# Moving every second low-part subtraction of the first block's weights from VectorE to GpSimd, in a two-block transformer kernel

## The chip, the cores and the metric

The kernel runs on one core of one Trainium2 chip. The metric is the device time of one execution in microseconds (us). Times below are the median of three runs; the profile is of one more execution.

## The reference, cut to what matters

Two transformer blocks are applied to 256 tokens of width 2048, everything in float32. The first block has adaptive scale and shift vectors, a projection `w_in` into attention and a recurrent mixer, two mixer projections that are gated and merged, the output projection `w_out`, and a gated feed-forward part. The second block prepends 16 tokens and has an attention layer and a gated linear attention layer.

```python
mod = (c @ w_ada[l] + b_ada[l])[:, None, :]
shift1, scale1, gate1, shift2, scale2, gate2 = jnp.split(mod, N_MOD, axis=-1)
h = rmsnorm(x, g_pre_mix[l]) * (1.0 + scale1) + shift1
proj = h @ w_in[l]
...
y_a = sliding_window_attention(qa, ka, va, attn_sinks[l]) @ w_attn_proj[l]
o_h = hgrn2_recurrence(q_h, f_h, i_h, lb_table[l])
...
merged = jax.nn.sigmoid(gate_a) * y_a + jax.nn.sigmoid(gate_h) * y_h
y = merged @ w_out[l]
x = x + gate1 * rmsnorm(y, g_post_mix[l])
...
y = (jax.nn.silu(g_ffn) * u_ffn) @ w_ffn_out[l]
x = x + gate2 * rmsnorm(y, g_post_ffn[l])
```

Every `@` with a large weight is the part that the change touches; the second block's weights are handled in the same way but are not touched.

## The kernel before, in words

**Weights as two parts.** TensorE multiplies in the reduced format fp32r, so each product is made of three: weight high part times activation high part, high times low, low times high (`mm3`, line 390). The weights come as a list of chunks, mostly 128 x 1024 float32 (512 KB), in the order of use (`_plan`, line 116): 56 chunks `w_first` and 92 chunks `w_in` (together the input projection), 32 `w_proj` (both mixer projections), 32 `w_out`, then the feed-forward part and the second block. So there are 212 chunks up to the end of the first block's output projection. Each chunk goes through three steps:

- `dma_chunks` (line 347): a DMA on SP's queue into one of five `raw` buffers (`NRAW`, line 53).
- `split_hi` (line 355): ScalarE rounds the chunk into one of three `wh` buffers (`NSPLIT`, line 62).
- `split_lo` (line 365): VectorE subtracts `wh` from `raw` and writes the low part into one of three `wl` buffers (lines 371 and 372). This is the last reader of the `raw` buffer, which then is free for another DMA.

**How far ahead.** A chunk of eight 128-deep tiles is 24 matmuls on TensorE. After the matmuls of a chunk are written down, `later_chunks` (line 384) writes down the low part of the chunk two further on, the high part of the chunk three further on, and the load of the one after that. A `wh` or `wl` buffer is free when TensorE has done with the chunk three before. The `raw` buffers are shared: the pieces of `w_adat` (128 of 512 KB, the adaptive vectors that are not needed at once) are loaded into the same five buffers (`later_load`, line 756), and VectorE reduces each with one multiply with accumulation against a broadcast copy of `c` (`later_piece`, line 767), then a few operations of one column.

**The order of the work.** Every engine executes its instructions in the order in which they are written down. The program writes them down with the help of a small model of the engines (`Clock`, line 144; `Timed`, line 191): matmuls of the main products first, and after each chunk `bg_step` (line 421) adds steps of the background work (the recurrence, the attention, gates, normalisations) as long as the model's VectorE is less than 4 us and its ScalarE less than 3 us ahead of its TensorE. A piece of `w_adat` is taken at a fixed rate for each chunk: 0.7 in the rest of `w_in`, 0.55 in `w_proj`, 0.85 in `w_out` (`RATES`, line 72), until there are none left. In the model a subtraction of 1024 elements on VectorE counts 1.14 us.

**Stages in the trace.** About 12 to 212 us: `w_first` with the first adaptive vectors; to 545 us the rest of `w_in` with recurrence and attention beside it; 545 to 637 us `w_proj` (`proj`, line 1343: two chunks for each of 16 outputs, two gated products read from PSUM, an addition and a split into high and low part on VectorE); 637 to 732 us `w_out`; then the feed-forward part begins with the first call of `next_layer` (line 1413).

**GpSimd before.** It does a few memsets and casts in the first block (lines 651, 691, 886, 955), small DMAs of the attention in the second block, and three additions at the end: the last loop (lines 2183 to 2197) makes eight tiles of the output, 128 x 512 each; tiles at k = 0, 4, 8 and 12 are summed by TensorE and copied by ScalarE, tiles at k = 2, 6 and 10 are added by GpSimd (line 2194), the tile at k = 14 by VectorE (line 2196).

Of the kernel before, what the change touches and what calls it, by code (L numbers as in the profile page):

```python
# [7 lines left out]
F32 = mybir.dt.float32  # L8
# [4 lines left out]
ALU = mybir.AluOpType  # L13
# [7 lines left out]
KT = D // 128  # L21
# [94 lines left out]
def _plan(a):  # L116

    plan = [a["w_first"][i] for i in range(a["w_first"].shape[0])]
    for i in range(74 - G1):
        plan += _tile_chunks(a["w_in"][i], KT)  # L120
    for n in range(KT):
        plan += _tile_chunks(a["w_proj"][n], KT)
    for n in range(KT):
        plan += _tile_chunks(a["w_out"][n], KT)
    plan += [a["w_fwave"][k] for k in range(KT)]
    i = 0
    for gi, gn in enumerate(FGROUPS):
        for j in range(2 * gn - (GF if gi == 0 else 0)):
            plan += _tile_chunks(a["w_ffn_in"][i], KT)
            i += 1  # L130
        for n in range(KT):
            plan += _tile_chunks(a[f"w_ffn_out{gi}"][n], gn)
    for w, wout in (("attn", "attn"), ("gla", "gla")):
        plan += [a[f"{w}_wave"][k] for k in range(KT)]
        for i in range(a[f"{w}_w_in"].shape[0]):
            plan += _tile_chunks(a[f"{w}_w_in"][i], KT)
        outs = [_tile_chunks(a[f"{w}_w_out"][n], KT) for n in range(KT)]
        if w == "attn":
            outs[:3] = [list(t) for t in zip(*outs[:3])]
        plan += sum(outs, [])  # L140
    return plan


class Clock:


    def __init__(self):
        self.t = dict(pe=0.0, dve=0.0, act=0.0, dma=0.0, dmaq=0.0)
        self.uses = {}
        self.end = 0.0  # L150
        self.table = None
# [70 lines left out]
def body(ctx, tc, a, out, dbg=None):  # L222
    nc = tc.nc
# [14 lines left out]
    def taken(pool, n, tile):  # L238

        r = rings.setdefault(pool, [])  # L240
        r.append(tile.tensor.name)
        if len(r) > n:
            clock.follow(r[-1], r[-1 - n])
        return tile

    def bank(name):
        return ps.tile([128, 512], F32, tag="b", name=name)
# [34 lines left out]
    clock = Clock()  # L282
    TE = Timed(nc.tensor, clock, "pe", lambda n, kw: n / 2400.0 * (
        4.0 if "lhsT" in kw and kw["lhsT"].dtype == F32 else 1.0) + 0.0025 if n > 16 else 0.11)
    VE = Timed(nc.vector, clock, "dve", lambda n, kw: max(0.07 + n / 960.0, 0.13))
    SE = Timed(nc.scalar, clock, "act", lambda n, kw: 0.1 + n / 1200.0)
    SY = Timed(nc.sync, clock, "dma", lambda n, kw: n * 512 / 390e3)
    GQ = Timed(nc.gpsimd, clock, "dmaq", lambda n, kw: DMAQ)
    tt = VE.tensor_tensor
    stt = VE.scalar_tensor_tensor  # L290
    ts = VE.tensor_scalar
    act = SE.activation
# [46 lines left out]

    plan = _plan(a)  # L340
    raws, splits = {}, {}
    ptr = dict(dma=0, hi=0, lo=0, use=0, mod=0)

    def raw_tile(name):
# [10 lines left out]
    def split_hi(upto):  # L355
        while ptr["hi"] < min(upto, len(plan)):
            i = ptr["hi"]
            n = plan[i].shape[1]
            dma_chunks(i + 1)
            wh = taken("wh", NSPLIT, whp.tile([128, CW], F32R, tag="wh", name="wh"))  # L360
            SE.copy(wh[:, :n], raws[i][:, :n])
            splits[i] = [wh, None]
            ptr["hi"] += 1

    def split_lo(upto):
        while ptr["lo"] < min(upto, len(plan)):
            i = ptr["lo"]
            n = plan[i].shape[1]
            split_hi(i + 1)
            wl = taken("wl", NSPLIT, wlp.tile([128, CW], F32R, tag="wl", name="wl"))  # L370
            tt(out=wl[:, :n], in0=raws.pop(i)[:, :n], in1=splits[i][0][:, :n].bitcast(F32),
               op=ALU.subtract)
            splits[i][1] = wl
            ptr["lo"] += 1

    def next_chunk():

        i = ptr["use"]
        ptr["use"] += 1
        split_lo(i + 1)  # L380
        split_hi(i + NSPLIT)
        return splits.pop(i)
# [13 lines left out]


    bg = []
    st_ = dict(quota=0.0, rate=0.0)

    limits = {}

# [37 lines left out]
    def mark(key):  # L440
        done[key] = clock.end
# [138 lines left out]
    def row_sums(st, sq, T, first, last):  # L580

        for i, o in enumerate(blocks(T)):
            TE.matmul(st[:, i:i + 1], lhsT=sq[:, o:o + 128], rhs=ones[:, 0:1],
                             start=(first and i == 0), stop=last, skip_group_check=True)
# [34 lines left out]
    def rstd_sums(accs, T, width, root=True, warm=0):  # L619
        st = bank("st")  # L620
        for i, acc in enumerate(accs):
            row_sums(st, acc, T, i == 0, i == len(accs) - 1)
        return rstd_rows(st, T, width, root, warm)

    def now(gen):

        while True:
            try:
                next(gen)
            except StopIteration as e:  # L630
                return e.value
# [596 lines left out]
    for i in range(n0):  # L1228
        u = ada_use()
# [20 lines left out]
    for gi, g in enumerate(KG):  # L1250
# [3 lines left out]
        for c in range(nch):  # L1254
            wh, wl = next_chunk()
# [42 lines left out]
            while used < int(want + 1e-6):  # L1298
# [8 lines left out]
                for _ in range(burst):  # L1307
                    u = ada_use()
# [104 lines left out]
    def next_layer(y, yacc, Ty, ycol, Tx, xcol, G, T, evac):  # L1413


        rb = now(rstd_sums(yacc, Ty, D, warm=WARM[0]))
        keep_warm(WARM[1])
        later_chunks()
        st = bank("xst")
        accs = [bank("wave") for _ in range(G)]  # L1420
        t0 = T2 - Tx

        def begin(k):
            if k >= KT:
                return
            residual(rb, y, Ty, ycol, k)
            if k:
                SE.mul(hh[k][:, :Tx], x[k][:, t0:], xcol(k))
            else:
                ts(out=hh[k][:, :Tx], in0=x[k][:, t0:], scalar1=xcol(k), scalar2=None,  # L1430
                   op0=ALU.mult)
                begin_lo(k)
            sqs[k] = t1("sq", Tx)
            act(out=sqs[k], in_=x[k][:, t0:], func=AF.Square)

        def begin_lo(k):
            if k < KT:
                pair_lo(hh[k][:, :Tx], hl[k][:, :Tx], x[k][:, t0:], xcol(k))

        def norm():  # L1440
            c = t1("sq", Tx)
            SE.copy(c, st[:, :Tx])
            yield 0.0
            rx = yield from rstd_sums([c], Tx, 32 * D)
            SE.copy(r2[:, :Tx], rx[:, :Tx])
            mark("r2")
            yield 0.0
            for g in range(G):
                while not room(evac, g):
                    yield 0.0  # L1450
                evac(g, accs[g][:, :T])
                wave["left"] -= 1
                yield 0.0

        del done["r2"]
        wave.update(left=G, most=G + 1)
        sqs = {}
        begin(0)
        begin(1)
        for k in range(KT):  # L1460
            wh, wl = next_chunk()
            tiles_ = [(accs[g][:, :T], slice(g * 128, (g + 1) * 128)) for g in range(G)]
            h, l = hh[k][:, :T], hl[k][:, :T]
            if k == 0:
                for w, v in ((wh, h), (wl, h), (wh, l)):
                    for o, ks in tiles_:
                        TE.matmul(o, lhsT=w[:, ks], rhs=v, start=w is wh and v is h, stop=False)
            else:
                for o, ks in tiles_:
                    mm3(o, wh[:, ks], wl[:, ks], h, l, False, k == KT - 1)  # L1470

            for j in range(k - 3, k + 1) if k % 4 == 3 else ():
                q = slice(32 * (j % 4), 32 * (j % 4) + 32)
                TE.matmul(st[q, :Tx], lhsT=ones[:, 0:32], rhs=sqs.pop(j), start=(k == 3),
                          stop=(k == KT - 1), skip_group_check=True)
            if k == KT - 1:
                urgent.append(norm())
                next(urgent[0])
            later_chunks()
            begin_lo(k + 1)  # L1480
            begin(k + 2)
# [180 lines left out]
    def turned(t, u):  # L1662

        for i in range(4):
            o, s = 32 * i, 32 * (i ^ 1)
            GQ.dma_start(out=u[o:o + 32], in_=t[s:s + 32])

# [488 lines left out]
    for i in range(G2, len(seq3)):  # L2156
        f, n, real = seq3[i]
# [8 lines left out]
    def x_pair(k):  # L2166
        return xs[k // 4][:, k % 4 * T2:(k % 4 + 2) * T2].rearrange(
            "p (a t) -> p a t", a=2)[:, :, R]
# [14 lines left out]
    for k in range(0, KT, 2):  # L2183
        if k == 4:
            sum_x(12)
        u = fin[k // 4][:, k % 4 * S:(k % 4 + 2) * S].rearrange("p (a t) -> p a t", a=2)
        tt(out=u, in0=rb, in1=y.two(k), op=ALU.mult)
        put = SY
        if k in sums:
            TE.matmul(sums[k], lhsT=ident, rhs=u, start=False, stop=True)  # L2190
            SE.copy(u, sums[k])
            put = nc.scalar
        elif k < KT - 2:
            nc.gpsimd.tensor_tensor(out=u, in0=u, in1=x_pair(k), op=ALU.add)
        else:
            tt(out=u, in0=u, in1=x_pair(k), op=ALU.add)
        put.dma_start(out=out[k // 2], in_=u)
# [160 lines left out]
```

## Time and profile before

| | |
|---|---|
| three runs, median (lowest to highest) | 2410.94 us (2409.06 to 2410.99) |
| the profiled execution, its own time | 2412.66 us |
| its span, first to last instruction | 2410.9 us |
| mean granted TensorE clock, share of full | 0.997 |
| TensorE, VectorE, ScalarE, GpSimd busy, share of the span | 99%, 70%, 50%, 3% |

PE is TensorE's matmuls, PEld its weight loads, DVE is VectorE, ACT is ScalarE, POOL is GpSimd and SP the engine whose queue issues the loads. In every view a time is in us from the start of the span, unless it is marked ns. A duration includes the tail of an instruction, so neighbours on one engine overlap a little in the records. A wait is given to whoever came last.

### The profile page before, as it was taken

Reading aid. Unit: us, or ns where it says so; the run is one execution under the profiler, and the core shown is the slowest. Engines: PE = TensorE matmul, PEld = TensorE weight load, DVE = VectorE, ACT = ScalarE, POOL = GpSimd, SP = SyncE. Lnnn points to the kernel's source line nnn. Section 1 sums busy time; section 2 is a strip of 40 time slices with the busy share of each in tenths; the row PEclk is TensorE's granted clock in tenths of the full one; section 3 lists DMA queues with packets and bytes.
Section 4 is the critical chain, followed back from the end, with each engine's and each line's share of the span. In section 5 each row is a group of like instructions: output and inputs, shape, how many; then the busy total and the mean of one; then the engine's idle time right before and its main releaser. Section 6 shows DMA issues by size and latency. Waiting matters only on the chain.

```text
span 2410.9 us, 49102 instructions
## 1 busy us (share of the span) xinstructions
PE 2380.5 (99%) x20217; PEld 2340.4 (97%) x20217; DVE 1691.1 (70%) x2865; ACT 1196.4 (50%) x1939; POOL 66.5 (3%) x131
## 2 busy tenths in 40 slices
PE   8999999999999999999999999999999999999998
PEld 7999999999999999999999999999999999999997
DVE  4897978888867965566655556777777566788664
ACT  4345565444445544444433444545555456855443
POOL 0000000000000000000000000121110000000000
PEclk9999999999999999999999999999999999999999
DMA  9975668798884666666665555554444445544453
GB/s 400 373 291 172 232 202 267 244 315 288 302 297 156 212 225 228 219 219 224 229 211 185 186 173 168 174 166 140 146 143 154 158 148 174 160 138 143 159 183 114
DMA packets 143249, 501.33 MB, mean 208 GB/s; under 512 B 17088, under 2 KB 17856, under 8 KB 143024
## 3 DMA queue, kind: packets, MB, share of 16 engines
q1 hardware_dynamic: 138240, 492.11, 60.7%
q0 software_dynamic: 3072, 3.35, 0.4%
q8 instruction: 158, 2.59, 0.4%
q10 hardware_dynamic: 1712, 2.73, 0.3%
q14 instruction: 67, 0.55, 0.1%
HBM read 492.68 MB, written 2.10 MB: 205 GB/s over the span
## 4 chain that ended last, share of the span: by engine, by line
PE 94%; DVE 2%; DMA 2%; ACT 1%; issue 0%; ACTq 0%; SPq 0%; DVEq 0%
PE acc L216 77%; PE wave L216 5%; PE yp L216 4%; DMA araw<-in_w_adat 1%; PE hgs L216 1%; PE sc L216 1%; PE go L216 1%; DVE wl L216 1%; PE ada L216 1%; PE st L216 1%; PE o L216 1%; DVE araw L216 1%; PE tp L216 0%; PE asc L216 0%; PE gm L216 0%
## 5 line engine op out<-in xcount | busy, mean ns | idle before, releaser
L216 ACT CAST wh<-raw 128x1024 fp32r<-128x1024 f32 (+1 forms) x754 | 774.0, 1027 | 1084.7 <-PE acc L216 732.1
L216 DVE TENSOR_TENSOR wl<-raw,wh 128x1024 fp32r<-128x1024 f32 (+1 forms) x754 | 899.7, 1194 | 432.9 <-ACT wh L216 429.3
L216 PE MATMUL acc<-hh,wh 128*128 128x256 f32 (+2 forms) x3488 | 1003.7, 288 | 2.5 <-ACT hh L216 2.5
L216 PE MATMUL acc<-hh,wl 128*128 128x256 f32 (+2 forms) x3488 | 988.5, 284 | 3.3 <-DVE wl L216 3.3
L216 PE MATMUL acc<-hl,wh 128*128 128x256 f32 (+2 forms) x3488 | 988.0, 284 | 2.9 <-DVE hl L216 2.9
L216 PEld LDWEIGHTS acc<-hh,wh 128*128 128x128 f32 x3488 | 658.8, 189 | 11.0 <-issue 5.0
L216 PEld LDWEIGHTS acc<-hl,wh 128*128 128x128 f32 x3488 | 658.3, 189 | 4.5 <-DVE hl L216 3.5
L216 PEld LDWEIGHTS acc<-hh,wl 128*128 128x128 f32 x3488 | 658.6, 189 | 4.1 <-DVE wl L216 4.1
L216 PE MATMUL acc<-h2l,wh 128*128 128x256 f32 x1200 | 337.9, 282 | 0.0
L216 PE MATMUL acc<-h2h,wl 128*128 128x256 f32 x1200 | 337.6, 281 | 0.0
L216 PE MATMUL acc<-h2h,wh 128*128 128x256 f32 x1200 | 335.8, 280 | 0.0
L216 PEld LDWEIGHTS acc<-h2h,wl 128*128 128x128 f32 x1200 | 227.3, 189 | 0.0
L216 PEld LDWEIGHTS acc<-h2h,wh 128*128 128x128 f32 x1200 | 226.9, 189 | 0.0
L216 PEld LDWEIGHTS acc<-h2l,wh 128*128 128x128 f32 x1200 | 225.2, 188 | 0.0
L216 DVE SCALAR_TENSOR_TENSOR araw<-araw,cb 128x1024 f32<-128x1024 f32 x144 | 175.5, 1219 | 12.9 <-DMA araw<-in_w_adat 12.7
L216 PE MATMUL wave<-hl,wh 128*128 128x272 f32 (+1 forms) x288 | 82.1, 293 | 0.8 <-DVE hl L216 0.8
L216 PE MATMUL wave<-hh,wh 128*128 128x272 f32 (+1 forms) x288 | 81.3, 291 | 0.1
L216 PE MATMUL wave<-hh,wl 128*128 128x272 f32 (+1 forms) x288 | 80.1, 287 | 0.0
L216 PE MATMUL acc<-oph,wh 128*128 128x272 f32 x256 | 74.3, 290 | 0.0
L216 PE MATMUL acc<-oph,wl 128*128 128x272 f32 x256 | 74.1, 289 | 0.0
L216 PE MATMUL acc<-opl,wh 128*128 128x272 f32 x256 | 73.7, 288 | 0.0
L216 PE MATMUL acc<-gpl,wh 128*128 128x256 f32 x256 | 72.1, 282 | 0.0
(390 smaller groups left out, 2987.5 us busy)
## 6 DMA issues: line engine op xcount, KB each, us to landing
raw<-in_w_ffn_in SPq DMA_DIRECT2D x164, 512.0 KB, 4.3
araw<-in_w_adat SPq DMA_DIRECT2D x128, 512.0 KB, 4.8
raw<-in_w_in SPq DMA_DIRECT2D x92, 512.0 KB, 4.8
raw<-in_gla_w_in SPq DMA_DIRECT2D x86, 512.0 KB, 3.6
raw<-in_attn_w_in SPq DMA_DIRECT2D x84, 512.0 KB, 3.5
araw<-in_w_mod SPq DMA_DIRECT2D x64, 512.0 KB, 9.2
raw<-in_w_ffn_out SPq DMA_DIRECT2D x64, 512.0 KB, 4.3
raw<-in_w_first SPq DMA_DIRECT2D x56, 512.0 KB, 6.8
```

The source lines that it names most:

```text
L216: return f(*args, **kw)
```

## The change

The subtraction of `split_lo` goes to GpSimd for chunks with an odd number, as long as a flag is set; the flag is cleared at the head of `next_layer`, whose first call comes after `w_out`. The program's model gets a sixth clock, for GpSimd, with 0.1 us + n/420 (2.54 us for 1024 elements). In the last loop the three additions of GpSimd go to VectorE.

```diff
     def __init__(self):
-        self.t = dict(pe=0.0, dve=0.0, act=0.0, dma=0.0, dmaq=0.0)
+        self.t = dict(pe=0.0, dve=0.0, act=0.0, dma=0.0, dmaq=0.0, pool=0.0)
...
     GQ = Timed(nc.gpsimd, clock, "dmaq", lambda n, kw: DMAQ)
+    GP = Timed(nc.gpsimd, clock, "pool", lambda n, kw: 0.1 + n / 420.0)
...
     raws, splits = {}, {}
+    st_ = dict(quota=0.0, rate=0.0, share=True)
     ptr = dict(dma=0, hi=0, lo=0, use=0, mod=0)
...
             wl = taken("wl", NSPLIT, wlp.tile([128, CW], F32R, tag="wl", name="wl"))
-            tt(out=wl[:, :n], in0=raws.pop(i)[:, :n], in1=splits[i][0][:, :n].bitcast(F32),
-               op=ALU.subtract)
+            e = GP if i % 2 and st_["share"] else VE
+            e.tensor_tensor(out=wl[:, :n], in0=raws.pop(i)[:, :n],
+                            in1=splits[i][0][:, :n].bitcast(F32), op=ALU.subtract)
             splits[i][1] = wl
...
     bg = []
-    st_ = dict(quota=0.0, rate=0.0)
...
     def next_layer(y, yacc, Ty, ycol, Tx, xcol, G, T, evac):
+        st_["share"] = False
         rb = now(rstd_sums(yacc, Ty, D, warm=WARM[0]))
...
             put = nc.scalar
-        elif k < KT - 2:
-            nc.gpsimd.tensor_tensor(out=u, in0=u, in1=x_pair(k), op=ALU.add)
         else:
             tt(out=u, in0=u, in1=x_pair(k), op=ALU.add)
```

## Rows read from the trace of the kernel before

**Rows 1.** The page: busy time, share of the span and instructions of each engine.

```profile
PE 2380.5 (99%) x20217; PEld 2340.4 (97%) x20217; DVE 1691.1 (70%) x2865; ACT 1196.4 (50%) x1939; POOL 66.5 (3%) x131
```

**Rows 2.** Busy time by stage (window length, PE, PEld, DVE, ACT, POOL, clock, DMA share, GB/s).

```profile
60.00:200.00 140.00, 136.24 (x1424) 132.12 (x1423) 122.38 (x199) 56.34 (x71) 2.66 (x4) 0.99 0.84 316
200.00:440.00 240.00, 239.80 (x2072) 234.37 (x2071) 203.56 (x360) 136.62 (x267) 1.58 (x3) 1.00 0.67 221
440.00:545.00 105.00, 105.00 (x888) 104.74 (x887) 85.42 (x144) 48.27 (x67) 0.00 (x0) 1.00 0.85 287
545.00:637.00 92.00, 92.00 (x780) 92.00 (x779) 83.02 (x140) 39.06 (x48) 0.00 (x0) 1.00 0.86 288
637.00:692.00 55.00, 52.00 (x433) 51.17 (x432) 41.24 (x63) 24.38 (x35) 0.00 (x0) 1.00 0.92 314
```

**Rows 3.** TensorE's waits, 0 to 800 us (total, times, longest).

```profile
PE acc L216 <- DVE wl L216: 3.3, 4, 1.1
PE acc L216 <- DVE hl L216: 2.9, 2, 2.8
```

**Rows 4.** ScalarE's and VectorE's order of time from 489 us (start, duration, instruction, idle before).

```profile
489.11 1.05 ACT L216 CAST wh<-raw 128x1024 fp32r<-128x1024 f32 x1 [1.79 <-PE acc L216]
...
494.79 1.05 ACT L216 CAST wh<-raw 128x1024 fp32r<-128x1024 f32 x1 [1.74 <-PE acc L216]
...
490.19 1.23 DVE L216 TENSOR_TENSOR wl<-raw,wh 128x1024 fp32r<-128x1024 f32 x1 [0.47 <-ACT wh L216]
491.33 0.48 DVE L216 SCALAR_TENSOR_TENSOR ohl<-gh,hgn,ohh 128x256 fp32r<-128x256 f32 x1
```

**Rows 5.** GpSimd's and VectorE's order of time at the end.

```profile
2398.05 3.74 POOL L2194 TENSOR_TENSOR fin<-fin,x 128x512 f32<-128x512 f32 x3 [163.78 <-DVE fin L216]
...
2396.67 4.87 DVE L216 TENSOR_TENSOR fin<-rb,y 128x512 f32<-128x512 f32 x8 [0.80 <-PE rb L216]
2401.58 0.76 DVE L216 TENSOR_TENSOR fin<-fin,x 128x512 f32<-128x512 f32 x1
```

**Rows 6.** GpSimd's and VectorE's order of time at 110 us.

```profile
110.08 0.40 POOL L886 CAST uc<-mask 128x256 uint8<-128x256 f32 x1
110.89 0.90 POOL L886 CAST uc<-mask 128x128 uint8<-128x128 f32 x1 [0.41 <-DMA mask<-in_uc]
...
109.83 0.68 DVE L216 TENSOR_TENSOR P<-acc,P 128x512 f32<-128x512 f32 x1
110.43 1.21 DVE L216 SCALAR_TENSOR_TENSOR araw<-araw,cb 128x1024 f32<-128x1024 f32 x1
...
111.57 1.30 DVE L216 TENSOR_TENSOR wl<-raw,wh 128x1024 fp32r<-128x1024 f32 x1
```

**Rows 7.** VectorE's groups, 545 to 637 us (count | busy, mean ns | idle before).

```profile
L216 DVE TENSOR_TENSOR wl<-raw,wh 128x1024 fp32r<-128x1024 f32 x33 | 40.3, 1221 | 1.8 <-ACT wh L216 1.7
L216 DVE SCALAR_TENSOR_TENSOR araw<-araw,cb 128x1024 f32<-128x1024 f32 x18 | 21.9, 1218 | 0.0
L216 DVE SCALAR_TENSOR_TENSOR t<-gat,yp 128x256 f32<-128x256 f32 x31 | 12.9, 418 | 7.3 <-PE yp L216 7.0
L216 DVE TENSOR_TENSOR t<-t,t 128x256 f32<-128x256 f32 x15 | 6.4, 426 | 0.5
L216 DVE SCALAR_TENSOR_TENSOR hl<-t,hh 128x256 fp32r<-128x256 f32 x15 | 6.3, 418 | 0.0
```

**Rows 8.** VectorE's groups, 440 to 545 us.

```profile
L216 DVE TENSOR_TENSOR wl<-raw,wh 128x1024 fp32r<-128x1024 f32 x34 | 41.6, 1224 | 10.2 <-ACT wh L216 10.2
L216 DVE SCALAR_TENSOR_TENSOR araw<-araw,cb 128x1024 f32<-128x1024 f32 x23 | 28.1, 1221 | 3.2 <-DMA araw<-in_w_adat 3.2
```

**Rows 9.** 637 to 692 us: ScalarE's longest wait, and a DMA group (count, size, us to landing).

```profile
ACT wh L216 <- DMA raw<-in_w_out: 22.4, 11, 4.8
...
raw<-in_w_out SPq DMA_DIRECT2D x17, 512.0 KB, 6.0
```

**Rows 10.** The chain that ended last, 2390 to 2411 us (start, us, what).

```profile
2402.97 0.59 ACT fin L216
```

## The prediction

> **What bounds the kernel now.** I read the busy times first. TensorE is busy for 99% of the span and VectorE for 70% [rows 1], so TensorE sets the time, and the change can only win back what TensorE loses by waiting up to `w_out`. The table by stage shows how little that is: between 60 and 692 us TensorE is idle for 3.8 us in the first window, 0.2 us in the second, nothing in the next two and 3.0 us in the last [rows 2], 7.0 us together. The list of waits agrees: TensorE waits 3.3 us for a low part, four times, and 2.9 us for other work of VectorE [rows 3]. The same table shows why somebody would want to relieve VectorE: it is busy for 75 to 90% of these windows, 83.0 of 92 us in the mixer projections [rows 2]. It is full, but its results come in time.
>
> How early they come is seen at 489 us. Two conversions by ScalarE, each released by TensorE at the end of a chunk, stand 5.68 us apart for two chunks, so a chunk takes 2.84 us. The subtraction that follows the first one ends at 490.19 + 1.23 = 491.42 us, and its chunk is used two chunks after the release, at about 489.1 + 5.7 = 494.8 us [rows 4]. The lead is 3.4 us.
>
> **The change part by part.** It takes 106 of the first 212 subtractions from VectorE (the odd ones up to `w_out`). From the start of a subtraction to the next instruction is 1.14 us [rows 4], so VectorE is freed of 106 x 1.14 = 121 us of 735.
>
> *Price of one on GpSimd.* The trace has no subtraction of 1024 elements there. The nearest rows are the three additions of 512 elements from two SBUF inputs: 3.74 us together, 1.25 us each [rows 5]. Twice that is 2.5 us; a fixed part of some 0.1 us is paid once and not twice (VectorE's eight products of 512 start 0.60 us apart [rows 5], and twice 0.60 is 0.06 more than 1.14). I take 2.4, with ends 2.3 and 2.6. The GPSIMD Engine Reference of the Trainium skill (section Elementwise — side-by-side cycle accounting) gives 4497 ns for 2048 elements, from which an estimate is 2.25 us; by it the GpSimd terms below would be 6% smaller.
>
> On its own that is harmless: 2.4 us in place of 1.23 leaves a lead of 2.2 us, and a pair of chunks lasts 5.68 us. What matters is whether GpSimd and VectorE can read at the same time.
>
> *The shared reading.* At 110 us three casts of GpSimd run beside VectorE. The first, of 256 elements, takes 0.40 us beside an addition with one PSUM input. The third, of half the elements, takes 0.90 us; it lies over the multiply of `araw`, which reads two SBUF tensors, and ends only after it. The subtraction that VectorE starts meanwhile takes 1.30 us instead of the usual 1.22 [rows 6, 7]. At the end of the kernel VectorE's addition from two SBUF tensors takes 0.76 us where GpSimd's last one is still running [rows 5]. So work with two SBUF inputs on VectorE and reading work on GpSimd take turns; an input from PSUM leaves GpSimd alone. These are single cases: ends are "no turns at all" and "GpSimd's time adds fully to VectorE's".
>
> The Trainium skill says this in SBUF — State Buffer, section Who interferes with whom: a VectorE instruction with two SBUF inputs contends with a GpSimd one that reads SBUF, and the loser blocks for the whole instruction. The rows show 0.08 us lost by VectorE, far from a whole GpSimd instruction, so they do not decide who waits; by the rule VectorE's queue would be held for up to 2.4 us each time, which is the third case below.
>
> *545 to 637 us.* Per row 33 subtractions, 18 multiplies of `araw`, 15 additions and 15 low parts of 256 elements read two SBUF tensors [rows 7]. After the change, with the 0.08 us by which neighbours overlap taken off each duration (1.14, 1.15 and 0.34 us): 16.5 x 1.14 + 18 x 1.15 + 30 x 0.34 = 49.7 us on VectorE, and 16.5 x 2.4 = 39.6 us on GpSimd. In turns that is 89.3 us, and 33 changes of hands at an estimated 0.1 us (about the gap from a release to a start in [rows 4]) make 92.6 of the 92 us that the window has. The 31 products from PSUM (31 x 0.34 = 10.5 us) and some 4 us of small operations stand in VectorE's queue in order, so they fall beside GpSimd only by luck. With half of them beside it, demand is 99.8 us: **+7 us**; ends 0 (all beside, changes of hands free) and +15 (none).
>
> *440 to 545 us.* 34 subtractions and 23 multiplies [rows 8]; the remaining 15.7 us of VectorE's 85.4 [rows 2, 8] are mostly two-input work, some 9 us. Demand is 17 x 1.14 + 23 x 1.15 + 9 + 17 x 2.4 + 3.4 = 99 us and half of the remaining 6: 102 of 105. **+1 us**, ends 0 and +3.
>
> *637 to 692 us.* Here the loads decide: ScalarE waits 22.4 us, 11 times, for a chunk of `w_out`, which lands 6.0 us after issue [rows 9], and the DMA engines are 92% busy [rows 2]. The five `raw` buffers are refilled in order when the low part (or the multiply of a piece) has read them. A subtraction on GpSimd holds its buffer 1.3 us longer, and 0.5 us more on average if it has to wait for a turn; the work behind it on VectorE is held 0.6 us on average (half a subtraction). With 9 of the first sort and 22 loads of the second in this window, that is 9 x 1.8 + 22 x 0.6 = 29 us of buffer time over five buffers, 6 us; a shorter landing time, with fewer loads on the way, gives back a little. **+5 us**, ends 0 and +9. The next load behind the late one on SP's queue waits with it, since the queue is in order.
>
> *60 to 440 us.* About 53 subtractions go over: GpSimd 53 x 2.4 = 127 us; VectorE's 326 us [rows 2] less 53 x 1.22, times 1.14/1.22 for the overlap in the records, is 244. Even with nothing beside each other that is 371 of 380 us. It fits in the mean; in the full stretch around 100 us it won't always. GpSimd's casts and memsets (the third cast waits for its load [rows 6]) now have a subtraction queued behind them, five or six times. **+3 us**, ends -4 (most of the 3.8 us idle goes, as VectorE is lighter) and +8. The model that writes the order no longer sees the 121 us on VectorE's clock and doesn't know about turns, so background work is written earlier; I price that at nothing, because the total stays, but it is why the upper ends are kept.
>
> *The last sums.* VectorE makes eight products at 0.60 us start to start [rows 5]. Three additions are now put among them, all ahead of the product for k = 12: 3 x 0.65 = 2.0 us later. Its product, the seventh, ended at about 2396.67 + 6 x 0.60 + 0.68 = 2400.95 us, and the last copy started at 2402.97 us [rows 5, 10]. Of the 2.0 us between, part is the sum and part is TensorE's queue of earlier sums; I take half for each, so that half of the 2.0 us later is hidden in the queue. GpSimd's path (end 2398.05 + 3.74 = 2401.79 us [rows 5]) was not the last. **+1 us**, ends 0 and +2.
>
> Sum: 7 + 1 + 5 + 3 + 1 = **+17 us**. Against the profiled execution (span 2410.9, own time 2412.66) that is 2429.7; the median of the runs lies 1.7 us lower, so 2410.94 + 17 = 2428 us. The ends of all terms add to -3 and +37.
>
> **Rivals.** A change of 0.2%, 4.8 us, is about what can be told from none.
>
> *No turns that matter (0.20).* The contention is as small as the 0.08 us of [rows 6], leads of 2 us absorb the rest, and TensorE never sees it. Then only the end remains: +1, 2412 us. For it speaks that TensorE waits nowhere between 200 and 637 us now; against it, the 0.90 us cast.
>
> *VectorE's relief is what counts (0.07), the other side.* In the two stretches that lose time, 60 to 200 and 637 to 692 us, the low parts come earlier because VectorE's queue is shorter by a subtraction for each pair, and buffers are freed earlier. It decides only if GpSimd's 2.4 us runs beside VectorE unhindered. At most the 7 us of idle come back, less 1 at the end: 2405 us.
>
> *VectorE held for whole instructions (0.18).* Each of 106 subtractions on GpSimd holds VectorE's queue for most of its time, PSUM work behind a held instruction too. Then VectorE's demand is its own plus 39.6 in 545 to 637 us (+15), +3 from 440, +9 from 637, +8 before 440, and the buffers of `araw`, freed late, slow the loads in the stretches at 85% DMA [rows 2] as well, for which I add a third of these 35: 12. With the end +48: 2459 us. The Trainium skill's rule leads to this case, and the 0.08 us of [rows 6] speaks against it.
>
> **The numbers.** Forecast 0.55, no effect 0.20, held 0.18, relief 0.07. The range reaches from 2410 (the no-effect case and the low ends) to 2450 (all upper ends, and half of the held case); outside are the relief and half of the held case, about 0.16. Faster by more than 0.2% is the relief alone, 0.07. The same: 0.20. Slower: 0.73. Within the forecast alone I would say 2417 to 2445.
>
> **What would show it.** If right: GpSimd has 106 subtractions with a mean well over 2.4 us (or VectorE's two-input work is longer than 1.22 us); TensorE waits for GpSimd's and VectorE's `wl`, most of it between 545 and 692 us, where its idle time grows by some 12 us; the last copy of ScalarE starts 7.3 us after the first product instead of 6.3 [rows 5, 10]. If TensorE's matmul count per window up to 637 us stays as it is, the turns are free and the second case holds. If low parts arrive in time and yet ScalarE waits longer for loads, the buffers are the cause and not the turns. The forecast is wrong at the root if GpSimd's mean is 2.4 us and VectorE's 1.22 as before.

## The result: 41 us slower, lost where the prediction saw room

The changed kernel takes 2452.03 us (median of four runs, 2450.06 to 2453.11) against 2410.97 for the kernel before beside it. The ratio is 1.0167, with a 95% interval of 1.0154 to 1.018: 41 us slower. The prediction said 2428, range 2410 to 2450. The sign is right; the size is more than twice what was forecast, and the measured time lies 2 us above the range.

The first lines of the page after. GpSimd's 106 subtractions are there, and VectorE is not less busy for it: 1701.1 us against 1691.1 [rows 1], although it was freed of 106 instructions of 1.2 us and got three short additions at the end.

```profile
span 2449.9 us, 49166 instructions
...
PE 2396.1 (98%) x20217; PEld 2349.9 (96%) x20217; DVE 1701.1 (69%) x2762; ACT 1195.8 (49%) x1939; POOL 338.1 (14%) x234
```

Busy time by stage after, in the windows of [rows 2]; the columns are the same.

```profile
60.00:200.00 140.00, 128.54 (x1340) 124.00 (x1339) 113.69 (x171) 51.08 (x64) 51.29 (x23) 0.98 0.81 301
200.00:440.00 240.00, 232.02 (x1941) 225.18 (x1940) 188.73 (x304) 132.09 (x261) 78.02 (x33) 0.97 0.61 202
440.00:545.00 105.00, 100.85 (x843) 99.36 (x841) 87.65 (x119) 43.20 (x61) 41.42 (x16) 1.00 0.76 250
545.00:637.00 92.00, 87.95 (x720) 86.93 (x721) 79.57 (x112) 37.75 (x51) 38.84 (x16) 0.98 0.82 284
```

Up to 440 us TensorE is now idle for 11.5 and 8.0 us; before it was 3.8 and 0.2 [rows 2]. That is the stretch for which the prediction had 3 us in all. Note VectorE in the second line: it is busy for 188.7 of 240 us, less than the 203.6 before, and yet TensorE loses time there.

The windows are cut by the clock, and the work in them shifts as the kernel gets later. Landmarks in the work say better how much is lost by when. These are the first and last start of three groups in the kernel before (count: shortest/median/longest in ns, first to last start): the gates `gat`, the mixer projections `yp`, and the first matmuls of the feed-forward part, `wave`.

```profile
L216 ACT ACTIVATE gat<-acc x32: 365/377/443, 268.4 to 546.9; 128x256 f32<-128x256 f32 x32
L216 PE MATMUL yp<-oah,wh x128: 276/280/290, 545.8 to 633.5; 128*128 128x256 f32 x128
L216 PE MATMUL wave<-hh,wh x288: 276/287/393, 736.4 to 2004.3; 128*128 128x272 f32 x96, 128*128 128x258 f32 x48
```

The same groups after.

```profile
L216 ACT ACTIVATE gat<-acc x32: 368/377/412, 286.3 to 580.9; 128x256 f32<-128x256 f32 x32
L216 PE MATMUL yp<-oah,wh x128: 277/280/415, 577.4 to 670.6; 128*128 128x256 f32 x128
L216 PE MATMUL wave<-hh,wh x288: 276/287/394, 778.5 to 2046.1; 128*128 128x272 f32 x96, 128*128 128x258 f32 x48
```

At the first gate 18 us are lost, at the first mixer projection 32, at the last one 37, at the feed-forward part 42. From there to the last sums nothing more is lost (`wave` ends 41.8 us later too). So 32 of the 42 us go before the mixer projections, 5.5 in them, and 5 in `w_out`.

**What TensorE waits for after**, 0 to 820 us (total, times, longest; before in [rows 3]):

```profile
PE acc L216 <- DVE wl L216: 10.1, 7, 2.5
PE acc L216 <- DVE hl L216: 8.4, 4, 5.0
...
PE acc L216 <- POOL wl L216: 5.1, 7, 1.2
PE yp L216 <- DVE wl L216: 2.7, 2, 2.0
PE acc L216 <- DVE P L216: 2.7, 1, 2.7
...
PE hgs L216 <- DVE R L216: 2.1, 2, 1.9
```

GpSimd's low parts are only 5.1 us of it. Of the waits that are new, nearly all the rest are for results of VectorE: its own low parts, `hl`, `P`, `R`. (A wait of 7.6 us for ScalarE's `t` at the start, left out here and in [rows 3], was 7.9 us before.) So it is mostly VectorE's results that come late. Between 60 and 440 us TensorE waits 13.2 us for `hl`, `P` and `R` together, 2.9 before, and 4.5 us for low parts, none before.

**Why VectorE is late** is seen in its groups, 0 to 800 us, of the kernel before (count | busy us, mean ns of one | idle before):

```profile
L216 DVE SCALAR_TENSOR_TENSOR araw<-araw,cb 128x1024 f32<-128x1024 f32 x112 | 136.5, 1219 | 12.9 <-DMA araw<-in_w_adat 12.7
...
L216 DVE TENSOR_TENSOR P<-acc,P 128x512 f32<-128x512 f32 x20 | 13.5, 686 | 4.8 <-PE acc L216 4.8
...
L216 DVE SCALAR_TENSOR_TENSOR mod<-mod,ada,vec 128x1 f32<-128x1 f32 x56 | 12.3, 219 | 2.0
```

The same groups after, with GpSimd's subtractions first:

```profile
L216 POOL TENSOR_TENSOR wl<-raw,wh 128x1024 fp32r<-128x1024 f32 x106 | 275.3, 2597 | 484.6 <-ACT wh L216 402.4 <-PE ada L216 23.9 <-DVE R L216 23.1
L216 DVE SCALAR_TENSOR_TENSOR araw<-araw,cb 128x1024 f32<-128x1024 f32 x112 | 176.0, 1572 | 19.3 <-DMA araw<-in_w_adat 17.6 <-issue 1.6
...
L216 DVE SCALAR_TENSOR_TENSOR mod<-mod,ada,vec 128x1 f32<-128x1 f32 x56 | 40.5, 723 | 2.0
...
L216 DVE TENSOR_TENSOR P<-acc,P 128x512 f32<-128x512 f32 x20 | 13.5, 686 | 14.1 <-PE acc L216 14.1
```

The multiplies of `araw` rise from 1219 to 1572 ns. The operation of a single column rises from 219 to 723 ns. Its shortest and median durations (218 and 220 ns) haven't moved, but its longest is 2322 ns:

```profile
L216 DVE SCALAR_TENSOR_TENSOR mod<-mod,ada,vec x56: 218/220/2322, 96.6 to 740.0; 128x1 f32<-128x1 f32 x56
```

So most of the 56 run as before, and some are held for about as long as a GpSimd subtraction takes. The additions to `P`, whose one input is in PSUM, stay at 686 ns. This time lies inside the records of VectorE; a reader who looks only for idle time doesn't find it.

**Two holds that reach TensorE.** VectorE's order of time after, at 118, 128 and 347 us (start, duration, instruction):

```profile
118.90 2.82 DVE L216 SCALAR_TENSOR_TENSOR araw<-araw,cb 128x1024 f32<-128x1024 f32 x1
...
128.74 2.74 DVE L216 SCALAR_TENSOR_TENSOR araw<-araw,cb 128x1024 f32<-128x1024 f32 x1
...
131.41 1.66 DVE L216 SCALAR_TENSOR_TENSOR hl<-hf,mod,hh 128x256 fp32r<-128x256 f32 x4
...
347.38 1.22 DVE L216 SCALAR_TENSOR_TENSOR araw<-araw,cb 128x1024 f32<-128x1024 f32 x1
...
348.64 2.22 DVE L216 SCALAR_TENSOR_TENSOR mod<-mod,ada,vec 128x1 f32<-128x1 f32 x1
...
353.26 0.42 DVE L216 TENSOR_TENSOR P<-hrb,P 128x256 f32<-128x256 f32 x1
```

GpSimd's order of time at the same places:

```profile
118.24 2.39 POOL L216 TENSOR_TENSOR wl<-raw,wh 128x1024 fp32r<-128x1024 f32 x1 [2.94 <-ACT wh L216]
128.05 2.34 POOL L216 TENSOR_TENSOR wl<-raw,wh 128x1024 fp32r<-128x1024 f32 x1 [7.42 <-ACT wh L216]
...
348.18 2.67 POOL L216 TENSOR_TENSOR wl<-raw,wh 128x1024 fp32r<-128x1024 f32 x1 [9.80 <-ACT wh L216]
```

GpSimd begins at 128.05 and ends at 130.39 us. VectorE's multiply begins at 128.74 and takes 2.74 us; less its usual 1.22 that is 1.52, nearly the 1.65 us to GpSimd's end. The low part `hl` of the activations stands behind it in VectorE's queue, and TensorE waits 5.0 us for it. At the same place it waited 2.8 us before [rows 3], so 2.2 of the 5.0 us are new. At 348.64 us the one-column operation takes 2.22 us, to within 0.01 us of GpSimd's end at 350.85. Behind it in the queue stands, after a low part and a multiply, the addition to `P` at 353.26 us, for which TensorE waits 2.7 us where it didn't wait before.

**What a stall costs on top.** TensorE has the same 20217 matmuls. Of the 39.0 us by which the span grew, 23.4 are idle time and 15.6 are more busy time (2396.1 against 2380.5 [rows 1]). After the longest stalls the granted clock falls to the lower of its two levels, 1.2 GHz:

```profile
350.00:355.00 5.00, 2.31 (x14) 1.96 (x13) 4.78 (x7) 5.00 (x19) 0.85 (x1) 0.81 0.79 256
355.00:360.00 5.00, 5.00 (x24) 4.71 (x24) 0.00 (x0) 2.09 (x7) 0.00 (x0) 0.51 0.69 252
```

In the first of these windows TensorE works 2.31 of 5 us, in the second without a gap, but at a granted clock of 0.51. The chain of the work that ended last shows the price: the 24 matmuls of a chunk take 5.49 us here and 2.83 us a little later.

```profile
353.74 5.49 PE acc L216 x24
...
360.93 2.83 PE acc L216 x24
```

In windows of 10 us from 60 to 780 us, the clock is below 0.97 in five (0.66, 0.83, 0.66, 0.83, 0.83). By an estimate of 10 us times what is missing to 1, that is at most 11.9 us; before it was two windows (0.91 and 0.92) and 1.7 us. So up to a quarter of the loss came behind the stalls and not in them. This accounts for at most 10.2 of the 15.6 us; where the rest of the added busy time comes from is left open.

### The profile page after: what moved, and what is told of

Its sections match the earlier page's. It is cut to its first block, busy times and chain, and to the rows that moved or that the text cites. A ratio compares the mean times of both kernels' runs of the same rounds, so it can differ in the third digit from the quotient of the medians.

```text
span 2449.9 us, 49166 instructions
## 1 busy us (share of the span) xinstructions
PE 2396.1 (98%) x20217; PEld 2349.9 (96%) x20217; DVE 1701.1 (69%) x2762; ACT 1195.8 (49%) x1939; POOL 338.1 (14%) x234
## 4 chain that ended last, share of the span: by engine, by line
PE 73%; DVE 8%; DMA 3%; issue 1%; ACT 1%; POOL 0%; SPq 0%; DVEq 0%; ACTq 0%; POOLq 0%
PE acc L216 61%; PE wave L216 5%; DVE araw L216 3%; DMA araw<-in_w_adat 2%; PE yp L216 1%; DVE wl L216 1%; DMA raw<-in_w_out 1%; PE sc L216 1%; PE go L216 1%; DVE mod L216 1%; DVE R L216 1%; DMA raw<-in_w_in 1%; PE o L216 1%; ACT wh L216 0%; PE tp L216 0%
## 5 line engine op out<-in xcount | busy, mean ns | idle before, releaser
L216 DVE TENSOR_TENSOR wl<-raw,wh 128x1024 fp32r<-128x1024 f32 (+1 forms) x648 | 779.7, 1204 | 419.0 <-ACT wh L216 412.9
L216 POOL TENSOR_TENSOR wl<-raw,wh 128x1024 fp32r<-128x1024 f32 x106 | 275.3, 2597 | 484.6 <-ACT wh L216 402.4
L216 DVE SCALAR_TENSOR_TENSOR araw<-araw,cb 128x1024 f32<-128x1024 f32 x144 | 215.0, 1493 | 19.3 <-DMA araw<-in_w_adat 17.6
L216 POOL DMA_DIRECT2D ru<-rt x32 | 15.8, 501 | 558.0 <-ACT rt L216 540.0
```

The lines of the kernel that those rows point to most:

```text
L216: return f(*args, **kw)
```

## The experiments

Twelve kernels, each with the median of its runs (4 to 11), and the ratio to the kernel before on the same chip with its 95% interval. "us" is the difference of the medians.

| run | what it is | ratio | us |
|---|---|---|---|
| e1 | before, with the new last sums | 0.9992 [0.9983, 1.0] | −1 |
| e2 | after, with the old last sums | 1.018 [1.0165, 1.0196] | +43 |
| e3 | after, in the old order of instructions | 1.0118 [1.0104, 1.0132] | +28 |
| e4 | before, plus idle reading by GpSimd | 1.0182 [1.0168, 1.0196] | +45 |
| e5 | before, plus idle writing by GpSimd | 1.0005 [0.9995, 1.0014] | +1 |
| e6 | after, GpSimd for chunks up to 148 only | 1.0128 [1.0111, 1.0145] | +30 |
| e7 | after, GpSimd for chunks from 148 only | 1.0028 [1.0018, 1.0038] | +7 |
| e8 | after, GpSimd writes and doesn't read | 1.002 [1.0012, 1.0029] | +5 |
| e9 | after's order, VectorE subtracts | 1.0019 [1.001, 1.0028] | +5 |
| e10 | after, every fourth chunk | 1.0065 [1.0051, 1.0078] | +15 |
| e11 | after, background planned later still | 1.029 [1.0274, 1.0306] | +68 |
| e12 | after, each subtraction in four pieces | 1.012 [1.0089, 1.0151] | +27 |

**Which half of the change?** e1 makes only the change of the last sums, e2 all but that.

```diff
-        elif k < KT - 2:
-            nc.gpsimd.tensor_tensor(out=u, in0=u, in1=x_pair(k), op=ALU.add)
```

> Only the last three additions go to VectorE; the subtractions stay as before. The prediction said +1 us (2412). The two traces show 14.2 us from the first product of the last sums to the end of the span before and 11.6 after, so the other view is -2 to -3 us (2408 to 2409).

> Only the subtractions go to GpSimd; the last sums stay as before. If the two parts are independent this is the changed kernel's 2452 less whatever the last sums bring alone: 2451 if they cost 1 us, about 2454.5 if they win 2.5.

e1 takes 2409.61 us against 2410.65, e2 2453.16 us. The last sums are worth about 1 us, between the two expectations, and a gain rather than the loss of 1 us that was forecast, though the interval reaches to no difference. The whole loss is that of the shared subtractions.

**Order, or the engines?** The changed kernel's planner keeps GpSimd's subtractions on a clock of their own and so writes background work earlier. e3 bills them to the model's VectorE, as before, so that all instructions stand in the order of before; only the engine differs.

```diff
-    GP = Timed(nc.gpsimd, clock, "pool", lambda n, kw: 0.1 + n / 420.0)
+    GP = Timed(nc.gpsimd, clock, "dve", lambda n, kw: max(0.07 + n / 960.0, 0.13))
```

> The changed kernel, but the program's model still bills the subtractions of GpSimd to VectorE at 1.14 us, so that every instruction stands where it stood before. If turns at reading are the cause: 2440 to 2455. If the background work that the model now writes down earlier is the cause: below 2425. If GpSimd's subtraction is merely late: as the changed kernel, 2452.

2438.66 us, just under the 2440 to 2455 expected of turns: 28 of the 41 us remain with the old order, and the other 13 need the new one. Its multiplies of `araw` take 1489 ns on average (1219 before, 1572 after):

```profile
L216 DVE SCALAR_TENSOR_TENSOR araw<-araw,cb 128x1024 f32<-128x1024 f32 x112 | 166.7, 1489 | 21.8 <-DMA araw<-in_w_adat 19.5 <-POOL wl L216 2.0 <-issue 0.2
```

**Is it GpSimd's reading?** e4 and e5 leave the kernel before as it is, all 212 subtractions on VectorE, and give GpSimd work whose results nobody uses, after every second one. In e4 it reads two SBUF inputs and writes to a spare tile:

```diff
+            if i % 2 and i < 212:
+                h = splits[i][0].bitcast(F32)
+                for j in range(0, CW, 256):
+                    nc.gpsimd.tensor_tensor(out=r2[:, :256], in0=h[:, j:j + 256],
+                                            in1=h[:, j:j + 256], op=ALU.subtract)
```

In e5 it reads one column and then only writes:

```diff
+            if i % 2 and i < 212:
+                nc.gpsimd.tensor_copy(r2[:, :1], splits[i][0][:, :1].bitcast(F32))
+                for _ in range(8):
+                    nc.gpsimd.memset(r2, 0.0)
```

> The kernel before, VectorE doing all its subtractions; beside it, for each odd chunk up to the output projection, GpSimd subtracts four pieces of 256 elements of the high part from themselves into a buffer that nobody reads there. Nobody waits for them. If turns at reading are the cause: at least 2430, more likely 2440 to 2490, as VectorE keeps its full work, with VectorE's two-input multiplies well over 1.22 us. If lateness or order is the cause: 2411, within 4.

> The control of the extra reads: the kernel before, and beside each odd chunk up to the output projection GpSimd reads one column of the high part and then fills a buffer that nobody reads there eight times (8 x 272 elements, some 2.6 us by the memset rows, no further reading). If it is turns at reading that cost the 45 us of the extra reads: 2411, within 4, and VectorE's multiplies stay at 1.22 us. If any work on GpSimd beside VectorE costs (a shared path for writes, or issue): 2430 or more.

Reading makes the kernel before slower by 45 us, to 2455.48 us, with no low part moved and the old order; more writing than that (2176 elements a chunk against 1024) costs nothing that can be told (2412.27 against 2411.46 us). One thing does wait for this work: the `wh` buffer that GpSimd reads is free only afterwards. ScalarE waits for that 18.5 us in e4 (9 times, longest 4.2) and 57.2 us in e5 (36 times, longest 3.1), where it costs nothing, so this doesn't explain the 45 us of e4. GpSimd's and VectorE's groups in e4, 0 to 800 us:

```profile
L376 POOL TENSOR_TENSOR r<-wh 128x256 f32<-128x256 f32 x424 | 446.0, 1052 | 308.5 <-ACT wh L216 282.3 <-ACT hh L216 0.5
...
L216 DVE SCALAR_TENSOR_TENSOR araw<-araw,cb 128x1024 f32<-128x1024 f32 x112 | 154.6, 1380 | 6.3 <-DMA araw<-in_w_adat 6.2
...
L216 DVE TENSOR_TENSOR wl<-raw,wh 128x1024 fp32r<-128x1024 f32 x212 | 291.1, 1377 | 25.3 <-ACT wh L216 24.0 <-PE ada L216 1.0
```

And in e5, where GpSimd is busy too, VectorE's multiplies stay at 1219 ns:

```profile
L376 POOL MEMSET r<- 128x272 f32 x848 | 276.5, 326 | 48.9
...
L216 DVE SCALAR_TENSOR_TENSOR araw<-araw,cb 128x1024 f32<-128x1024 f32 x112 | 136.5, 1219 | 15.0 <-DMA araw<-in_w_adat 14.8
```

**Is it the later low part, then, or the buffers?** e8 keeps the changed kernel's order and all waits, but GpSimd fills the low part with zeros: one column read from `wh`, three fills, one column from `raw`, 2.9 us together on average. The low parts of these 106 chunks are left out.

```diff
+                nc.gpsimd.tensor_copy(wl[:, :1], wh[:, :1])
+                nc.gpsimd.memset(wl.bitcast(F32), 0.0)
+                nc.gpsimd.memset(wl[:, :768].bitcast(F32), 0.0)
+                nc.gpsimd.memset(wl[:, :512].bitcast(F32), 0.0)
+                nc.gpsimd.tensor_copy(wl[:, :1], raw[:, :1])
```

e9 keeps the order too and gives all subtractions back to VectorE; only the model still bills every second one to GpSimd.

```diff
+                clock.issue("pool", 0.1 + n / 420.0, [wl[:, :n]], [raw, wh])
+                nc.vector.tensor_tensor(out=wl[:, :n], in0=raw, in1=wh, op=ALU.subtract)
```

> The changed kernel with the same order and the same waits, but GpSimd fills the low part of an odd chunk with zeros instead of subtracting (one column read from the high part first, three fills of 1024, 768 and 512 elements, one column read from the chunk last), some 2.3 to 2.6 us as before. So the low parts of these 106 chunks are left out of the sums. Same lateness, same order of work, VectorE relieved of the same 106 subtractions, but hardly any reading by GpSimd. If turns at reading cause the loss: 2405 to 2414, the low end if VectorE's relief is worth what the second rival said. If GpSimd's late low parts or the later release of the loaded buffers cause it: 2435 or more.

> The order of the changed kernel, but VectorE does all subtractions as before. The changed kernel came out 13 us slower than the same kernel in the old order. If that order is bad in itself, because the model forgets the subtractions of odd chunks: 2418 to 2430. If the order hurts only together with turns at reading: 2409 to 2414 (the last sums are those of the changed kernel).

Both take nearly the same time, 2416.56 and 2416.68 us, 5 us more than before; both miss their expected ranges by some 3 us (e8 2405 to 2414, e9 2409 to 2414 or from 2418). So the later result, the later release of the `raw` buffers, the new order and the relief of VectorE come to 5 us together (e8), and the new order alone to 5 us (e9): without turns, nothing near 41 us. The page of e8 shows the relief that the changed kernel doesn't get, 1577.8 us busy, and the multiplies are at 1220 ns. With the same 2762 instructions on VectorE the changed kernel has 1701.1 us: 123.3 us more, an estimate of 1.16 us of holding for each of GpSimd's 106 subtractions.

```profile
PE 2382.7 (99%) x20217; PEld 2340.6 (97%) x20217; DVE 1577.8 (65%) x2762; ACT 1195.9 (50%) x1939; POOL 368.7 (15%) x658
...
L216 DVE SCALAR_TENSOR_TENSOR araw<-araw,cb 128x1024 f32<-128x1024 f32 x112 | 136.6, 1220 | 37.2 <-DMA araw<-in_w_adat 26.4 <-POOL wl L377 3.6 <-POOL wl L380 2.5
```

The 5 us of the two are not the same 5 us. The landmarks, e8 first and e9 below:

```profile
L216 PE MATMUL yp<-oah,wh x128: 276/280/290, 546.3 to 634.0; 128*128 128x256 f32 x128
L216 PE MATMUL wave<-hh,wh x288: 276/287/393, 743.3 to 2011.0; 128*128 128x272 f32 x96, 128*128 128x258 f32 x48
...
L216 PE MATMUL yp<-oah,wh x128: 278/280/290, 552.4 to 641.1; 128*128 128x256 f32 x128
L216 PE MATMUL wave<-hh,wh x288: 276/287/393, 743.6 to 2011.4; 128*128 128x272 f32 x96, 128*128 128x258 f32 x48
```

Against the kernel before, e9 is 6.6 us late at the first mixer projection and loses nothing in `w_out`: that is the order by itself, written by a model that forgets 106 subtractions. e8 has the same order and is only 0.5 us late up to the last mixer projection, so VectorE's relief seems to make up for the order there; then it loses 6.4 us in `w_out`, where TensorE waits 5.7 us for GpSimd's late low parts. These are readings of one execution each, and `w_out` varies: in e1 and e5, which move no low part, it took about 2 us less than in the kernel before. With 28 us for the turns in the old order and 5 for the order without turns, about 8 of the 41 us are left for the two together.

**Where?** e6 shares only up to chunk 148 (the input projection), e7 only from there on (`i >= 148` in the same place), e10 every fourth chunk (`i % 4 == 3`).

```diff
-            e = GP if i % 2 and st_["share"] else VE
+            e = GP if i % 2 and i < 148 and st_["share"] else VE
```

> The changed kernel with GpSimd's subtractions for chunks below 148 only (the input projection). The prediction's terms give this part +4 us and the last sums 0: 2415. The landmarks of the changed kernel's trace (first matmul of the mixer projections 31.6 us later) give 2440 to 2444 if the stages are independent.

> The changed kernel with GpSimd's subtractions for chunks from 148 on only (mixer projections and output projection). The prediction's terms 7 + 5 give 2422; the landmarks give 37.1 - 31.6 + 5.0 = 10.5 us: 2421. If the loss there was only carried over from a late start: 2411 to 2414.

> The changed kernel with every fourth subtraction on GpSimd instead of every second. If each turn costs a little by itself, half of 41: 2430 to 2434. If the loss comes where VectorE's queue is full and vanishes with some room: below 2422. If a few first turns already cost most: above 2440.

The early part costs 30 us and the late one 7, together 37 of the 41. e6 came out as expected from the landmarks; e7's 2418.22 us lies between its two expectations. Half the shared chunks (e10) cost 15 us, clearly less than half; 2426.43 us is between the first two cases of its expectation. No share was found that gains. The mixer projections, e6 first and e7 below:

```profile
L216 PE MATMUL yp<-oah,wh x128: 277/280/283, 576.1 to 663.9; 128*128 128x256 f32 x128
...
L216 PE MATMUL yp<-oah,wh x128: 276/280/290, 545.2 to 632.9; 128*128 128x256 f32 x128
```

They last 87.8 and 87.7 us, as long as before (87.7). So e7, where GpSimd shares in them, loses nothing in them; its `wave` begins 5.2 us late, all of it from `w_out`. The 5.5 us that the changed kernel loses in the mixer projections come only when both parts are shared; why is left open.

**A planner that knows.** If the background is written too early, one could bill each of GpSimd's subtractions to the model's VectorE at the 2.15 us for which it may be held.

```diff
+    GP = Timed(nc.gpsimd, clock, "dve", lambda n, kw: 0.1 + n / 500.0)
```

> The changed kernel, with the program's model billing each subtraction of GpSimd to VectorE as 2.15 us, as if VectorE were held for most of it, so that background work is written down later than before the change. If the order matters through VectorE's full queue, this beats the old order's 2438.7: 2418 to 2432. If room in the queue doesn't help: 2436 to 2445.

It is the slowest of all, 2479.92 us, where either case expected 2445 at the most. The trace shows where: at 500 to 540 us TensorE has nothing to do for 30% of the time, while the loads are nearly idle too (last column but one, the DMA share: 0.15 and 0.25) and the granted clock, the column before it, is 0.57 and 0.83.

```profile
500.00:520.00 20.00, 12.65 (x60) 11.99 (x61) 9.45 (x14) 5.33 (x10) 0.97 (x2) 0.57 0.15 54
520.00:540.00 20.00, 15.24 (x101) 13.75 (x101) 8.80 (x25) 4.40 (x6) 2.40 (x1) 0.83 0.25 78
```

By the program, background that is put off must be written down at once where a later stage needs it, and then there are few chunks to hide it. That reading of the window wasn't tested by a run of its own.

**Sum of the reading, or length of a hold?** e12 writes each of GpSimd's subtractions as four of 256 elements, in the changed kernel's order.

```diff
+                for j in range(0, n, 256):
+                    nc.gpsimd.tensor_tensor(out=wl[:, j:j + 256], in0=raw[:, j:j + 256],
+                                            in1=wh[:, j:j + 256], op=ALU.subtract)
```

> The changed kernel, with each subtraction on GpSimd written as four of 256 elements, in the same place of the order; the order of all other work is the changed kernel's. If what costs is the length of a single hold (a small operation of VectorE waiting out an instruction of 2.4 us), pieces of 0.6 us hold it a quarter as long: VectorE's one-column accumulations fall from a mean of 0.72 us to about 0.35, TensorE's waits for hl and P go, and the time is about 2425 to 2435. If what costs is the sum of GpSimd's reading, in pieces or whole, VectorE gets a turn no sooner or loses as much in all, and the time is 2448 to 2465; the pieces on GpSimd would then have a mean of about 1 us, as the dummy reads had, so that the low parts of the odd chunks come up to 2 us later.

2438.68 us (four runs, 2436 to 2450), between what the two theories expected. The groups of e12, 0 to 800 us:

```profile
L377 POOL TENSOR_TENSOR wl<-raw,wh 128x256 fp32r<-128x256 f32 x424 | 396.7, 966 | 354.0 <-ACT wh L216 311.4 <-PE acc L216 16.0 <-PE ada L216 12.3
L216 DVE SCALAR_TENSOR_TENSOR araw<-araw,cb 128x1024 f32<-128x1024 f32 x112 | 159.1, 1421 | 43.9 <-DMA araw<-in_w_adat 38.1 <-POOL wl L377 3.4 <-DMA raw<-in_w_out 2.4
...
L216 DVE SCALAR_TENSOR_TENSOR mod<-mod,ada,vec 128x1 f32<-128x1 f32 x56 | 24.9, 445 | 2.0
```

The pieces take 0.97 us each, 3.7 us for a chunk in place of 2.6: now GpSimd waits for more turns, and VectorE for shorter ones (445 instead of 723 ns for one column). That takes away 14 of the 41 us, though the interval (+21 to +36 us) leaves it open between 5 and 20. So the length of a hold matters and the sum of the reading does too. In e4, with the same pieces, VectorE had kept its 106 subtractions, and that was as slow as the change.

## Why the prediction was right and wrong

**Right: the mechanism's sort.** "So work with two SBUF inputs on VectorE and reading work on GpSimd take turns; an input from PSUM leaves GpSimd alone" is what e4 and e5 show, and VectorE's work with a PSUM input is left alone as well: 686 ns before and after.

**Near in number, not shown in mechanism: the late stages.** The mixer projections lost 5.5 us (+7 was predicted) and `w_out` 5 (+5 was predicted), by the landmarks. The +7 stood for VectorE and GpSimd filling the stage in turns; e7 has these turns there (GpSimd's 16 subtractions, VectorE busy for 77 of 88 us) and loses nothing, so that the number came near is luck. In `w_out` a loss without turns was right: e8 loses 6.4 us there. Whether it is the buffers, as predicted, or the late low parts is not shown. TensorE's waits were to be for low parts, most of them from 545 to 692 us; there it waits 4.2 us for them, and the longest waits that grew were for `hl` and `P`, before 440 us.

**Right in kind: GpSimd's price.** 2.4 us was taken. The ones that began before VectorE's multiply took 2.34 and 2.39 us; the mean of 2.60 includes GpSimd's own waits.

**Wrong: 60 to 440 us, "It fits in the mean".** The step added the busy times of both engines, 371 of 380 us, and concluded +3. Together with +1 for 440 to 545 us that made 4 us up to the mixer projections. The landmarks say 32, and e6 alone 30. The sum was no measure of this: in 200 to 440 us VectorE was busy for 188.7 of 240 us and TensorE still lost 8 us. A hold of up to 2.3 us in a queue that runs in order delays whatever stands behind it. From 60 to 440 us that was mostly `hl`, `P` and `R`, for which TensorE waits 13.2 us, against 4.5 us for low parts with their lead of 3.4 us. The lead was measured for one sort of result and taken for all; and over the whole first block the low parts lost their lead too, with waits of 18.3 us in place of 3.3.

**Wrong: "The rows show 0.08 us lost by VectorE, far from a whole GpSimd instruction, so they do not decide who waits", and then 0.18 for the held case.** The rows didn't decide it, but the sum went on as if they had, by turns without long holds. One instance, in which VectorE's instruction began 0.2 us before the end of a short cast, can't show how long it would wait for a long one. The one-column operations show it here: up to 2.3 us for one that takes 0.22. The Trainium skill's rule (SBUF — State Buffer, section Who interferes with whom: a two-input VectorE instruction and a reading GpSimd one lock each other out, for the whole instruction) held, and this trace agrees with it, on PSUM inputs also.

The rival in which VectorE is held for whole instructions, 2459 us, came nearest, 7 us off; but its parts were not right either: it had most of its loss from 440 to 692 us and only 8 us before.

**Wrong: the order "priced at nothing, because the total stays".** The order alone costs 5 us (e9), and with the turns, by difference, some 8 more.

**Missing: a term for the clock.** Each stall was priced at its own length. By the estimate above, matmuls at the lower clock cost at most 11.9 us, against 1.7 before: up to 10 of the 41 us.

**Small, and by e1's median wrong in sign: the last sums.** The copy did come later after the first product, as predicted (7.3 us): 2445.97 − 2438.29 = 7.7 us, 6.3 before. But the span then ends 3.0 us after the issue of the last output DMA has ended, where before it was 7.0. The end of the chain and ScalarE's last copy:

```profile
2438.29 1.30 DVE fin L216 x2
...
2445.97 0.58 ACT L216 COPY fin<-sum 128x512 f32<-128x512 f32 x1 [1.34 <-PE sum L216]
```

Why the end is shorter is left open; no run asked for it.

**Slips in the working.** They change little: 99.8 us of demand in 92 is +7.8, not +7; the low ends add to −4, not −3; and the gap from a release to a start in [rows 4] is 0.03 us, not 0.1, which would make the changes of hands 1.0 us in place of 3.3.

## What to carry to other kernels

Before work goes to GpSimd to relieve a busy VectorE, ask what both read: 106 reading instructions of 2.4 us beside work with two SBUF inputs cost 41 us (28 in the old order), while as long a time of fills, which only write, cost nothing that could be told. These traces suggest pricing such a move by the longest single hold in front of the operation with the least lead, and not by busy sums, and adding the matmuls that run at the lower clock behind each stall; no run here tested such a price ahead of time. Where an engine's busy time doesn't fall when work is taken away, compare the mean and the longest duration of its smallest operations (the median stayed the same here): they show holds that no list of waits names.

## Not expected of the hardware

- A VectorE operation of one column, 0.22 us, was recorded with up to 2.3 us beside a GpSimd subtraction, 0.72 on average over 56. The time held is inside the recorded duration.
- Shorter pieces on GpSimd share better: with 256 elements each, the one-column operations were held to a mean of 0.45 us, while GpSimd's own time for a chunk grew from 2.6 to 3.7 us.
- GpSimd's fills, 848 of 272 elements at 326 ns, left VectorE's multiplies at 1219 ns.
